# Output projections with each tile's evacuation one product later, full and partial tiles in turn, and VectorE in source order in layer A

## The chip, the core and the metric

One core of one Trainium2 chip runs the whole program. The metric is device time in microseconds (us) of one execution. Five engines work from queues of their own: TensorE (PE in the profile, its weight loads PEld), VectorE (DVE), ScalarE (ACT), GpSimd (POOL) and SyncE (SP), which issues most DMAs.

## What is computed

One inference step of a two-layer decoder over 1024 prompt tokens and 8 sample tokens. Layer A mixes tokens with a gated recurrence, layer B with sliding-window attention; both add a cross-attention into memory tokens. Around the change only this part of each layer matters:

```python
mix = jnp.concatenate([tok_out, x_out], axis=-1) @ w_out[l]
h = h + rms_norm(mix, norm_post_mix[l])
u = jnp.square(jax.nn.relu(rms_norm(h, norm_pre_mlp[l]) @ w_up[l]))
h = h + rms_norm(u @ w_down[l], norm_post_mlp[l])
```

The first line is the output projection. Width is 1024, so `w_out` has 8 output tiles of 128 features and 8 inner blocks of 128.

## The kernel before

Activations lie with features on the partitions. The 1032 tokens are cut into NCH = 3 chunks of CH = 344 columns. `X` holds the input of the current product, split into a high and a low part, so each inner block costs three matmuls (`mm3`, lines 287 to 289). A **full** tile of the projection is 8 blocks, 24 matmuls. A **partial** tile (`rest`) takes only the blocks that an earlier stage left out and is added to what that stage put into `Y[m]`: in layer A the two blocks LATE = (4, 5), 6 matmuls, for tiles 0 to 3; in layer B three blocks, 9 matmuls, for tiles 0 to 3 of chunks 0 and 1 (in chunk 2 all tiles are full).

A product lands in a PSUM bank and must be evacuated before the bank is used again. A full tile is evacuated by ScalarE (`A.copy` to `Y[m]`), a partial tile by VectorE (`tt(V, y, y, ps, add)`). Behind either stands `sumsq`: ScalarE squares the tile (line 221), and VectorE or GpSimd adds the square to the chunk's sums. Banks: layer A's projection takes "ax" (4 banks) and "dn" (2) in turn, layer B's only "dn".

After the last tile of a chunk, `post_norm` puts 12 pieces of work into the list `bg`: `stat` (loads of the residual `h`, matmuls of line 177 over the sums, square root, reciprocal, `spread`), `stat_b` (the matmul of line 197 that gives the scale to all partitions), eight `step(k)` and `stat_next` (line 177 again, over the squares of the new residual). `tick()` runs the next pieces: 1.5 of them after each tile of the following chunk, so that the norm of chunk c is traced among the products of chunk c + 1. The norm of the last chunk is traced among the first products of the MLP (`mlp`, `dense_chunk` with `up_ev`, line 1067), which read the X that the steps write, chunk by chunk. One step is this:

```python
V.scalar_tensor_tensor(y, y, gain(gpost, k), box["r"], op0=ALU.mult, op1=ALU.mult)
tt(V if k % 4 == 3 else G, y, y, h, ALU.add)
...
A.activation(h, y, AF.Square)
if k % 4 and not direct:
    r = row(k - k % 4)
    tt(V if k < 4 else G, r, r, h, ALU.add)
...
split_gain(y, gain(nxt, k), hi, lo)
```

`split_gain` is a ScalarE copy with a scale (hi) and a VectorE operation that subtracts it (lo).

A scheduler orders each engine's instructions by their readiness in its own estimate of time and by source order; where `ordered[0]` is set, the wrapper `InOrder` pins each VectorE instruction behind the one traced before it on VectorE. Before, it is set only inside `mlp`. Operations through `tt` are recorded on line 51 (VectorE) or line 98 (GpSimd).

Of the kernel before, what the change touches and what calls it, by code (L numbers as in the profile page):

```python
# [13 lines left out]
ALU = mybir.AluOpType  # L14
# [4 lines left out]
KT = D // P  # L19
# [3 lines left out]
CH = 344  # L23
NCH = 3
# [3 lines left out]
G_MEM, G_LB, G_HG, G_KV, G_PREMIX, G_POSTMIX, G_PREMLP, G_POSTMLP = 0, 16, 22, 28, 36, 52, 68, 84  # L28
# [6 lines left out]
def trunk_kernel(ctx, tc, xT, memT, wia, wib, wkk, wkv, wmk, wo, wu, wd, cmk, cmv, sth, ssk, ssv,  # L35
# [3 lines left out]
    ordered = [False]  # L39
# [15 lines left out]
    V, A, T, G, S = nc.vector, nc.scalar, nc.tensor, nc.gpsimd, nc.sync  # L55
    V = InOrder(V)
# [28 lines left out]
    def const(shape, name, src=None, dt=F32):  # L85
        t = cpool.tile(list(shape), dt, name=name, tag=name)
        if src is not None:
            S.dma_start(t, src)
        return t
# [7 lines left out]
    def tt(eng, out, a, b, op):  # L97
        return eng.tensor_tensor(out, a, b, op=op)  # L98
# [16 lines left out]
    def cs(c):  # L115
        return slice(c * CH, (c + 1) * CH)
# [99 lines left out]
    def sumsq(acc, src, first, eng):  # L216
        if first:
            A.activation(acc, src, AF.Square)
        else:
            sq = chunk_tile(acc.shape[-1])  # L220
            A.activation(sq, src, AF.Square)
            tt(eng, acc, acc, sq, ALU.add)
# [75 lines left out]
    def dense_mm(w, c, ks=range(KT), bank=None):  # L298
        ps = (psum(bank) if bank else dense_bank())[:, :CH]
        ks = list(ks)  # L300
        for i, k in enumerate(ks):
            mm3(ps, w[0][:, k * P:(k + 1) * P], w[1][:, k * P:(k + 1) * P], X[:, k, 0, cs(c)], X[:, k, 1, cs(c)],
                i == 0, i == len(ks) - 1)
        return ps

    def dense_chunk(w, c, evac, ks=range(KT)):
        evac(c, dense_mm(w, c, ks))
# [559 lines left out]
    def tick(n=1.5):  # L867
        due[0] += n
        while due[0] >= 1:
            due[0] -= 1  # L870
            if bg:
                bg.pop(0)()

    u2 = const([RB, N // RB], "u2")
    u4 = const([RB, N // RB], "u4")

    def post_norm(Y, a, w, acc, gpost, hsrc, hdst, nxt, scaled, bank="ac", rbank="ax", direct=False):

        hts, box = [], {}
        per = N // w
        sl, bl = slice(a, a + w), slice(a // RB, (a + w) // RB)

        def row(k):
            return hts[k // per][:, k % per]

        def stat():
            for i, k0 in enumerate(range(0, KT, per)):  # L890
                ht = slot("p" if i < 2 else "t", (P, per, w))
                n = min(per, KT - k0)
                for src, o in rows(hsrc, k0, n, a, w):
                    S.dma_start(ht[:, :n, o], src)
                hts.append(ht)
            st = rstd_tok(acc, square=u4[:, bl] if scaled else None, bank=rbank)
            if scaled:
                tt(V, st, st, u2[:, bl], ALU.mult)
            box["r"] = spread(st)

        def stat_b():
            box["r"] = bcast(box["r"], bank)

        def step(k):
            y, h = Y[k][:, sl], row(k)
            V.scalar_tensor_tensor(y, y, gain(gpost, k), box["r"], op0=ALU.mult, op1=ALU.mult)
            tt(V if k % 4 == 3 else G, y, y, h, ALU.add)
            for dst, o in rows(hdst, k, 1, a, w):
                S.dma_start(dst, y[:, o].unsqueeze(1))
            if nxt is None:  # L910
                return
# [4 lines that stand above are left out]
            hi, lo = X[:, k, 0, sl], X[:, k, 1, sl]  # L916
            if scaled:
                split(y, hi, lo, G if k % 4 == 1 else V)
            else:
                split_gain(y, gain(nxt, k), hi, lo)  # L920

        def stat_next():
            if nxt is None:
                return
            st = rstd_tok(*(row(k) for k in range(0, KT, 1 if direct else 4)), bank=rbank)
            if scaled:
                box["n"] = spread(st)
            else:
                tt(V, u2[:, bl], st, st, ALU.mult)
                tt(V, u4[:, bl], u2[:, bl], u2[:, bl], ALU.mult)  # L930

        def next_b():
            if nxt is not None and scaled:
                A.copy(nxt[:, sl], bcast(box["n"], bank))
        bg.extend([stat, stat_b] + [lambda k=k: step(k) for k in range(KT)] + [stat_next, next_b])
# [36 lines left out]
    def out_late(l, box, ws, hsrc, hdst):  # L972
        Y = box["Y"]
        accs = slot("t", (P, NCH, CH))
        Y += [slot(t) for t in ("q", "q", "k", "k")]

        def full(m, c):
            def ev(c, ps):
                A.copy(Y[m][:, cs(c)], ps)
                sumsq(accs[:, c], Y[m][:, cs(c)], m == ME, G if m % 2 else V)  # L980
            dense_chunk(ws[1 + m - ME], c, ev, ks=EARLY + LATE)

        def rest(m, c):
            ps = dense_bank()[:, :CH]
            w = ws[0]
            for i, k in enumerate(LATE):
                o = m * 256 + i * P
                mm3(ps, w[0][:, o:o + P], w[1][:, o:o + P], X[:, k, 0, cs(c)], X[:, k, 1, cs(c)], i == 0, i == 1)
            y = Y[m][:, cs(c)]
            tt(V, y, y, ps, ALU.add)  # L990
            sumsq(accs[:, c], y, False, V if m % 2 else G)

        wide[0] = True
        for c in range(NCH):
            for m in (4, 5, 6, 7, 0, 1, 2, 3):
                (full if m >= ME else rest)(m, c)
                tick()
            post_norm(Y, c * CH, CH, accs[:, c], G_POSTMIX + 8 * l, hsrc, hdst, G_PREMLP + 8 * l, False)
        return Y

    def out_b(hsrc, hdst):


        Y, ws, held, seen, box = {}, {}, {}, set(), {}
        first = EARLY[:5]

        def load(c, ks):
            for k in ks:
                n = CH if c < NCH - 1 or k > 5 else NP_ - c * CH
                t = held[k, c] = chunk_tile(n)  # L1010
                S.dma_start(t, mixs[k][:, c * CH:c * CH + n])

        def put(c, ks):
            for j, k in enumerate(ks):
                t = held[k, c]
                put_x(k, slice(c * CH, c * CH + t.shape[1]), t, G if j else V)

        def weight(m, tags=None):
            ws[m] = load_folded(12 + m, tags)

        def out(m):
            if m not in Y:
                Y[m] = slot("k" if m < 2 or m > 3 else "c")
            return Y[m]

        def stat(m, c):
            if "acc" not in box:
                box["acc"] = slot("r", (P, NCH, CH))
            sumsq(box["acc"][:, c], Y[m][:, cs(c)], c not in seen, V if m % 2 else G)
            seen.add(c)  # L1030

        def early(m, c):
            dense_chunk(ws[m], c, lambda c, ps: A.copy(out(m)[:, cs(c)], ps), ks=first)

        def rest(m, c):
            y = Y[m][:, cs(c)]
            tt(V, y, y, dense_mm(ws[m], c, EARLY[5:] + LATE), ALU.add)
            stat(m, c)

        def full(m, c):  # L1040
            dense_chunk(ws[m], c, lambda c, ps: A.copy(out(m)[:, cs(c)], ps), ks=EARLY + LATE)
            stat(m, c)

        def norm(c):
            post_norm([Y[m] for m in range(KT)], c * CH, CH, box["acc"][:, c], G_POSTMIX + 8, hsrc, hdst,
                      G_PREMLP + 8, False)
        return load, put, weight, early, rest, full, norm, Y
# [848 lines left out]
    def at(i, f, *args):  # L1896
        fill.setdefault(i, []).append(lambda: f(*args))
# [25 lines left out]
        for f in fs:  # L1923
            at(i, f)
    for i, f, m, c in ((23, early, 0, 0), (24, early, 1, 0), (25, early, 2, 0), (26, early, 0, 1), (27, early, 1, 1), (28, early, 2, 1), (29, early, 3, 0), (30, early, 3, 1), (29, rest, 0, 0), (30, rest, 1, 0), (30, rest, 2, 0), (31, rest, 3, 0), (32, full, 4, 0)):
        at(i, f, m, c)
    for i, *h in parts:
        at(i, load, *h)
    run_groups(groups, fill)
    weight(6, ("c", "c"))  # L1930
    weight(7, ("r", "r"))
    for c in range(NCH):
        for m in (*range(3, KT), *range(3)):
            if c or m > 4:
                (full if m > 3 or c == 2 else rest)(m, c)
                tick()
        norm(c)
    mlp(1, hs[2], yT, None, [YB[m] for m in range(KT)])
    tick(len(bg))

# [101 lines left out]
```

## Time and profile before

| what | value |
|---|---|
| median of 3 runs | 2524.55 us (2521.96 to 2527.94) |
| the profiled execution | 2523.64 us |
| its span | 2521.5 us |
| TensorE busy | 2342.8 us |
| VectorE busy | 1757.5 us |
| GpSimd busy | 1435.6 us |
| ScalarE busy | 1108.2 us |
| mean granted TensorE clock | 0.969 |

The span runs from the first to the last instruction of the profiled execution; 2.1 us of its time lie around it. Matmuls are pipelined, so a busy TensorE is not one at its peak. The output projection of layer A lies at about 580 to 653 us of the span, that of layer B at about 1,740 to 1,812 us.

### The profile page before, as it was taken

What the parts mean: (1) busy time and instruction counts of PE and PEld (TensorE: products, weight loads), DVE (VectorE), ACT (ScalarE), POOL (GpSimd) and SP (SyncE); (2) the same over time, 40 slices, a digit from 0 to 9 for tenths busy, and PEclk for the clock granted to TensorE, in tenths of its full rate; (3) what the DMA queues carried; (4) which work ended last, traced back from release to release, by engine and by line L of the source; (5) the groups of instructions that cost most, each with busy time, mean ns of one, the idle gap of its engine ahead of it and who ended that gap; (6) DMA issues with size and microseconds to landing.
All of it is one profiled execution on the core that took longest, in us unless ns stands there. A gap on an engine that the chain in (4) does not pass through costs nothing. (4 is left out here: it accounts for less than half of the span.)

```text
span 2521.5 us, 45361 instructions
## 1 busy us (share of the span) xinstructions
PE 2342.8 (93%) x17055; PEld 2261.5 (90%) x17055; DVE 1757.5 (70%) x2813; ACT 1108.2 (44%) x2457; POOL 1435.6 (57%) x1130
## 2 busy tenths in 40 slices
PE   7998999989899999999999998889999999899997
PEld 6887989989799999899998987778999999899997
DVE  7778677775768887567657466775577887567847
ACT  6573434444443333444344364565443333344424
POOL 4546453453686664557765344443576666457846
PEclk9999999999899999999999999889999999999998
DMA  4435455522335557655563333334334556755482
GB/s 160 134 103 183 159 186 160 169 86 91 107 118 177 175 184 240 191 161 151 194 213 106 118 88 114 101 94 148 109 105 157 184 173 202 257 147 153 127 280 75
DMA packets 231928, 383.01 MB, mean 152 GB/s; under 512 B 28106, under 2 KB 118794, under 8 KB 231692
## 3 DMA queue, kind: packets, MB, share of 16 engines
q1 hardware_dynamic: 154524, 253.80, 30.1%
q10 hardware_dynamic: 77184, 126.31, 17.2%
q8 instruction: 134, 2.20, 0.4%
q14 instruction: 86, 0.70, 0.1%
HBM read 253.27 MB, written 123.56 MB: 149 GB/s over the span
## 5 line engine op out<-in xcount | busy, mean ns | idle before, releaser
L287 PE MATMUL dn<-X,ws 128*128 128x344 f32 (+2 forms) x1136 | 374.2, 330 | 31.5 <-DVE X L51 10.7
L288 PE MATMUL dn<-X,ws 128*128 128x344 f32 (+2 forms) x1136 | 369.7, 325 | 0.0
L289 PE MATMUL dn<-X,ws 128*128 128x344 f32 (+2 forms) x1136 | 368.6, 324 | 0.0
L98 POOL TENSOR_TENSOR ws<-wr,ws 128x512 fp32r<-128x512 f32 (+1 forms) x118 | 223.6, 1897 | 160.8 <-ACT ws L225 146.4
L287 PEld LDWEIGHTS dn<-X,ws 128*128 128x128 f32 x1136 | 219.6, 193 | 42.3 <-DVE X L51 22.0
L51 DVE TENSOR_TENSOR X<-ws,X 128x516 fp32r<-128x516 f32 x160 | 172.7, 1088 | 105.8 <-ACT X L225 105.7
L288 PEld LDWEIGHTS dn<-X,ws 128*128 128x128 f32 x1136 | 219.9, 194 | 2.0 <-issue 0.8
L289 PEld LDWEIGHTS dn<-X,ws 128*128 128x128 f32 x1136 | 219.9, 194 | 1.2 <-issue 0.4
L287 PE MATMUL ax<-X 128*128 128x258 f32 x736 | 209.6, 286 | 9.9 <-DVE k L51 6.5
L288 PE MATMUL ax<-X 128*128 128x258 f32 x736 | 211.2, 287 | 4.2 <-POOL X L98 4.2
L289 PE MATMUL ax<-X 128*128 128x258 f32 x736 | 210.4, 286 | 0.0
L225 ACT CAST ws<-wr 128x1024 fp32r<-128x1024 f32 (+1 forms) x138 | 116.1, 844 | 132.8 <-DMA wfd<-ws 36.6
L98 POOL TENSOR_TENSOR p<-p,sm 128x512 f32<-128x512 f32 (+2 forms) x92 | 87.8, 977 | 130.4 <-DVE sm L51 72.8
L225 ACT CAST X<-ws 128x516 fp32r<-128x516 f32 (+1 forms) x192 | 109.6, 621 | 107.8 <-PE ax L289 45.6
L287 PEld LDWEIGHTS ax<-X 128*128 128x128 f32 x736 | 141.1, 192 | 10.9 <-DVE k L51 7.0
L287 PE MATMUL ax<-X,ws 128*128 128x344 f32 (+2 forms) x472 | 147.7, 314 | 2.6 <-DVE X L51 2.6
L289 PE MATMUL ax<-X,ws 128*128 128x344 f32 (+2 forms) x472 | 146.3, 310 | 0.0
L288 PEld LDWEIGHTS ax<-X 128*128 128x128 f32 x736 | 141.8, 193 | 5.0 <-POOL X L98 5.0
L288 PE MATMUL ax<-X,ws 128*128 128x344 f32 (+2 forms) x472 | 145.5, 308 | 0.0
L289 PEld LDWEIGHTS ax<-X 128*128 128x128 f32 x736 | 141.7, 193 | 0.0
L287 PE MATMUL ac<-X 128*128 128x258 f32 x496 | 139.5, 283 | 1.7 <-ACT k L1234 1.7
L288 PE MATMUL ac<-X 128*128 128x258 f32 x496 | 140.5, 284 | 0.0
(649 smaller groups left out, 8271.0 us busy)
## 6 DMA issues: line engine op xcount, KB each, us to landing
ws<-u ACTq DMA_DIRECT2D x160, 258.0 KB, 2.7
u<-k SPq DMA_DIRECT2D x104, 258.0 KB, 3.0
wr<-wu ACTq DMA_DIRECT2D x104, 256.0 KB, 3.3
wfd<-ws SPq DMA_DIRECT2D x20, 1024.0 KB, 5.1
X<-u21s SPq DMA_DIRECT2D x32, 516.0 KB, 6.8
ct<-u ACTq DMA_DIRECT2D x112, 129.0 KB, 2.8
u<-k SPq DMA_DIRECT2D x104, 129.0 KB, 2.3
u21s<-mv SPq DMA_DIRECT2D x26, 516.0 KB, 3.6
```

Source lines behind the costliest of these rows:

```text
L51: r = f(*args, **kw)
L98: return eng.tensor_tensor(out, a, b, op=op)
L225: A.copy(hi, src)
L287: T.matmul(ps, wh, xl, start=first, stop=False, skip_group_check=more)
L288: T.matmul(ps, wl, xh, start=False, stop=False, skip_group_check=more)
L289: T.matmul(ps, wh, xh, start=False, stop=last, skip_group_check=more)
```

## The change

Evacuation becomes a function of its own. `full` and `rest` now issue the matmuls and return the evacuation; the new `one_late` runs each evacuation after the next tile's matmuls have been traced, and then `tick()`. `norm(c)` is held back with the evacuation of the chunk's last tile, so it too stands behind the first product of the next chunk. Tiles go (4, 0, 5, 1, 6, 2, 7, 3) in place of (4, 5, 6, 7, 0, 1, 2, 3) in layer A and (3, 4, 5, 6, 7, 0, 1, 2) in layer B, where chunk 0 has only tiles 5, 6 and 7 left. In layer A `ordered[0]` is set for the whole of the three chunks, the steps of the norms of chunks 0 and 1 among them; in layer B it is not. The number of operations and their engines stay.

```diff
+    def one_late(o, steps):
+        ordered[0] = o
+        held = []
+        for f in steps:
+            if held and f.__defaults__[0] is None:
+                held.append(f)
+                continue
+            new = f()
+            for g in held:
+                g()
+            held = [new]
+            tick()
+        for g in held:
+            g()
+        ordered[0] = False
...
         def full(m, c):
-            def ev(c, ps):
+            ps = dense_mm(ws[1 + m - ME], c, EARLY + LATE)
+
+            def ev():
                 A.copy(Y[m][:, cs(c)], ps)
                 sumsq(accs[:, c], Y[m][:, cs(c)], m == ME, G if m % 2 else V)
-            dense_chunk(ws[1 + m - ME], c, ev, ks=EARLY + LATE)
+            return ev
...
-            y = Y[m][:, cs(c)]
-            tt(V, y, y, ps, ALU.add)
-            sumsq(accs[:, c], y, False, V if m % 2 else G)
+
+            def ev():
+                y = Y[m][:, cs(c)]
+                tt(V, y, y, ps, ALU.add)
+                sumsq(accs[:, c], y, False, V if m % 2 else G)
+            return ev
...
-        for c in range(NCH):
-            for m in (4, 5, 6, 7, 0, 1, 2, 3):
-                (full if m >= ME else rest)(m, c)
-                tick()
-            post_norm(Y, c * CH, CH, accs[:, c], G_POSTMIX + 8 * l, hsrc, hdst, G_PREMLP + 8 * l, False)
+        one_late(True, [(lambda m=m, c=c: (full if m >= ME else rest)(m, c)) if m is not None else lambda m=None, c=c: norm(c)
+                  for c in range(NCH) for m in (4, 0, 5, 1, 6, 2, 7, 3, None)])
...
-    for c in range(NCH):
-        for m in (*range(3, KT), *range(3)):
-            if c or m > 4:
-                (full if m > 3 or c == 2 else rest)(m, c)
-                tick()
-        norm(c)
+    one_late(False, [(lambda m=m, c=c: (full if m > 3 or c == 2 else rest)(m, c)) if m is not None
+              else lambda m=None, c=c: norm(c)
+              for c in range(NCH) for m in (4, 0, 5, 1, 6, 2, 7, 3, None) if c or m is None or m > 4])
```

In layer B `full`, `rest` are changed in the same way; its early tiles, run during the attention, still evacuate at once.

## Rows read from the trace of the kernel before

**Rows 1.** The page, busy time, share of the span and instructions of each engine.
```profile
PE 2342.8 (93%) x17055; PEld 2261.5 (90%) x17055; DVE 1757.5 (70%) x2813; ACT 1108.2 (44%) x2457; POOL 1435.6 (57%) x1130
```

**Rows 2.** Stretches of layer A: busy time (x instructions) of PE, PEld, DVE, ACT, POOL; clock.
```profile
596.10:622.20 26.10, 24.17 (x158) 23.67 (x156) 17.33 (x27) 12.35 (x29) 12.82 (x13) 1.00 0.20 68
622.20:653.30 31.10, 21.89 (x125) 20.89 (x125) 23.28 (x35) 16.01 (x35) 19.86 (x15) 0.79 0.49 166
653.30:687.00 33.70, 31.83 (x198) 30.70 (x198) 23.00 (x36) 12.61 (x28) 17.95 (x18) 0.94 0.24 79
```

**Rows 3.** TensorE's waits, 575 to 700 us: us in total, times, longest.
```profile
PE ax L177 <- DVE p L51: 5.9, 2, 3.9
PE dn L287 <- DVE k L51: 5.3, 1, 5.3
```

**Rows 4.** TensorE in order of time, layer A: start, us, instruction.
```profile
601.13 0.70 PE L177 MATMUL ax<-ones,t 128*86 128x1 f32 x8
...
606.02 0.74 PE L197 MATMUL ac<-ct,ones 86*128 86x344 f32 x2
...
612.40 0.32 PE L287 MATMUL ax<-X,p 128*128 128x344 f32 x1
...
616.20 0.32 PE L287 MATMUL dn<-X,ws 128*128 128x344 f32 x1
...
686.99 0.43 PE L287 MATMUL ax<-X,ws 128*128 128x344 f32 x1 [0.79 <-DVE X L51]
```

**Rows 5.** VectorE in order of time, layer A: evacuation, statistics, steps.
```profile
593.49 0.51 DVE L51 TENSOR_TENSOR k<-k,ax 128x344 f32<-128x344 f32 x1 [3.13 <-PE ax L289]
...
602.16 0.17 DVE L51 RECIPROCAL sm<-sm 86x4 f32<-86x4 f32 x1 [4.12 <-ACT sm L183]
602.37 0.51 DVE L51 TENSOR_TENSOR ct<-ident,sm 86x344 f32<-86x344 f32 x1
606.80 2.02 DVE L51 SCALAR_TENSOR_TENSOR k<-k,gn,ac 128x344 f32<-128x344 f32 x4 [3.93 <-PE ac L197]
...
613.99 0.57 DVE L51 SCALAR_TENSOR_TENSOR X<-k,gn,X 128x344 fp32r<-128x344 f32 x1
...
636.34 2.02 DVE L51 SCALAR_TENSOR_TENSOR k<-k,gn,ac 128x344 f32<-128x344 f32 x4 [3.91 <-PE ac L197]
...
668.58 2.02 DVE L51 SCALAR_TENSOR_TENSOR k<-k,gn,ac 128x344 f32<-128x344 f32 x4 [3.93 <-PE ac L197]
...
685.34 1.59 DVE L51 SCALAR_TENSOR_TENSOR X<-k,gn,X 128x344 fp32r<-128x344 f32 x1
```

**Rows 6.** ScalarE and GpSimd in order of time: square root, addition, square, hi part.
```profile
601.87 0.26 ACT L183 ACTIVATE sm<-ax,eps 86x4 f32<-86x4 f32 x1 [0.82 <-PE ax L177]
...
606.86 0.93 POOL L98 TENSOR_TENSOR t<-t,ct 128x344 f32<-128x344 f32 x1 [9.44 <-ACT ct L221]
...
608.71 0.49 ACT L912 ACTIVATE p<-k 128x344 f32<-128x344 f32 x1 [1.93 <-POOL k L98]
609.11 0.57 ACT L229 ACTIVATE X<-k,gn 128x344 fp32r<-128x344 f32 x1
```

**Rows 7.** DMA issues, 590 to 700 us: KB each, median us to landing.
```profile
p<-xT SPq DMA_DIRECT2D x4, 516.0 KB, 6.1
```

**Rows 8.** GpSimd's split of a weight and VectorE beside it, in order of time.
```profile
645.24 2.63 POOL L98 TENSOR_TENSOR ws<-wr,ws 128x1024 fp32r<-128x1024 f32 x1
...
645.58 2.66 DVE L51 TENSOR_TENSOR p<-p 128x344 f32<-128x344 f32 x1
```

**Rows 9.** Layer B, in order of time: an evacuation by VectorE, and TensorE.
```profile
1769.37 0.50 DVE L51 TENSOR_TENSOR k<-k,dn 128x344 f32<-128x344 f32 x1
1769.55 0.42 PE L177 MATMUL ax<-ones,p 128*86 128x1 f32 x2 [5.06 <-issue]
...
1770.27 0.49 PE L288 MATMUL dn<-X,ws 128*128 128x344 f32 x1
1770.55 0.49 PE L289 MATMUL dn<-X,ws 128*128 128x344 f32 x1
```

More of the change, by code (lines that the diff above doesn't have):

```diff
@@ L988, in rest, with norm @@
                 mm3(ps, w[0][:, o:o + P], w[1][:, o:o + P], X[:, k, 0, cs(c)], X[:, k, 1, cs(c)], i == 0, i == 1)
-            y = Y[m][:, cs(c)]
-            tt(V, y, y, ps, ALU.add)
-            sumsq(accs[:, c], y, False, V if m % 2 else G)
-        wide[0] = True
-        for c in range(NCH):
-            for m in (4, 5, 6, 7, 0, 1, 2, 3):
-                (full if m >= ME else rest)(m, c)
-                tick()
-            post_norm(Y, c * CH, CH, accs[:, c], G_POSTMIX + 8 * l, hsrc, hdst, G_PREMLP + 8 * l, False)
+            def ev():
[3 more added lines that the diff above has]
+            return ev
+        def norm(c):
+            post_norm(Y, c * CH, CH, accs[:, c], G_POSTMIX + 8 * l, hsrc, hdst, G_PREMLP + 8 * l, False)
+        wide[0] = True
+        one_late(True, [(lambda m=m, c=c: (full if m >= ME else rest)(m, c)) if m is not None else lambda m=None, c=c: norm(c)
+                  for c in range(NCH) for m in (4, 0, 5, 1, 6, 2, 7, 3, None)])
         return Y
@@ L1035, in rest, with ev @@
         def rest(m, c):
-            y = Y[m][:, cs(c)]
-            tt(V, y, y, dense_mm(ws[m], c, EARLY[5:] + LATE), ALU.add)
-            stat(m, c)
-        def full(m, c):
-            dense_chunk(ws[m], c, lambda c, ps: A.copy(out(m)[:, cs(c)], ps), ks=EARLY + LATE)
-            stat(m, c)
+            ps = dense_mm(ws[m], c, EARLY[5:] + LATE)
+            def ev():
+                y = Y[m][:, cs(c)]
+                tt(V, y, y, ps, ALU.add)
+                stat(m, c)
+            return ev
+        def full(m, c):
+            ps = dense_mm(ws[m], c, EARLY + LATE)
+            def ev():
+                A.copy(out(m)[:, cs(c)], ps)
+                stat(m, c)
+            return ev
         def norm(c):
@@ L1925, in trunk_kernel @@
     for i, f, m, c in ((23, early, 0, 0), (24, early, 1, 0), (25, early, 2, 0), (26, early, 0, 1), (27, early, 1, 1), (28, early, 2, 1), (29, early, 3, 0), (30, early, 3, 1), (29, rest, 0, 0), (30, rest, 1, 0), (30, rest, 2, 0), (31, rest, 3, 0), (32, full, 4, 0)):
-        at(i, f, m, c)
+        at(i, f if f is early else lambda f, *a: f(*a)(), *(() if f is early else (f,)), m, c)
     for i, *h in parts:
```

## The prediction

> **What bounds the kernel now.** The page comes first: TensorE is busy 93% of the span [rows 1], so a change that adds and removes no work can only move TensorE's idle stretches and the moment from which it runs without a gap. The stretches of layer A come next: from 596.1 to 687.0 us, 90.9 us, TensorE is busy 24.17 + 21.89 + 31.83 = 77.9 us, 13.0 us idle, and in the middle stretch its granted clock is 0.79 [rows 2]. TensorE's waits name what is late: 5.9 us in two waits of line 177 (the statistics of the new residual, `stat_next`) for VectorE, and 5.3 us in one wait for a bank that VectorE has not evacuated [rows 3]. In layer B one wait of line 177 takes 5.06 us, put down to "issue"; VectorE's instruction that starts 0.18 us before its end, an evacuation of a partial tile, shows which queue was behind [rows 9]. So 16 us of TensorE's idle time hang on VectorE.
>
> They are not all a gain, though. Follow VectorE in layer A: the first scaling of the three norms starts at 606.80, 636.34 and 668.58, and the last lo part of the third ends at 685.34 + 1.59 = 686.93 [rows 5]; TensorE, in the third chunk of the MLP's first products, is waiting for it and goes on at 686.99 [rows 4]. From there it runs without a wait. Layer A's time is therefore set by when VectorE ends the third norm; TensorE reaching that point sooner only waits longer. In layer B the stretch after the 5.06 us wait is TensorE's own, and a wait removed there is kept.
>
> **Layer A, part by part.** The later evacuation and the new order add no operation. Two things change for the chain of norms.
>
> First, `stat_b` now has a partial tile in front of it in source order, where a full one stood. Four partial tiles take 616.20 - 612.40 = 3.80 us, so a partial tile costs 0.95 and a full one, four times the matmuls, 3.80 [rows 4]. From line 177 to line 197 it is 606.02 - 601.13 = 4.89 us now; 2.85 less gives 2.04, about what the chain between needs: 0.70 for the matmuls, 0.26 square root, 0.17 reciprocal, 0.51 spread [rows 4, 5, 6]. The first norm starts at 606.80 - 2.85 = 603.95.
>
> Second, VectorE's source order. Before, VectorE did all eight scalings in a row and the lo parts behind them, while GpSimd and ScalarE worked on the steps between. Pinned, the lo part of step k stands ahead of the scaling of step k + 1, so a step runs as a chain: scaling 0.51 (2.02 for four), addition on GpSimd 0.93, square 0.40 (608.71 to 609.11, when ScalarE takes the next), hi part 0.57, lo part 0.57 [rows 5, 6]; with four hand-overs of about 0.03 us 3.1 us. The two steps whose addition is VectorE's own take 0.51 in place of 0.93: 2.7. Eight steps: 6 x 3.1 + 2 x 2.7 = 24.0 us. Between them stand the evacuations: two of 0.5, one addition of 0.5, and one that also waits for ScalarE's square, 0.5 + 0.49 + 0.5 = 1.5 (an evacuation is 0.51 [rows 5]): 3.0. Together 27.0 us.
>
> Then `stat_next`: 16 matmuls of line 177, twice the 0.70, square root, reciprocal and two small products of about 0.16: 2.15; and the last partial tile with its square, 1.5. The next norm's sums are then ready, and `stat` and `stat_b` take 0.70 + 0.26 + 0.17 + 0.51 + 0.74 = 2.4. By this sum a period is 27.0 + 2.15 + 1.5 + 2.4 = 33.05. The residual's loads give more: their places are free only when `stat_next` has read the squares in them, and they land 6.1 us after the issue [rows 7], ahead of the first addition: 27.0 + 1.4 + 6.1 - 0.5 = 34.0. I take 34.0, since the next norm now follows at once; the periods before were 29.54 and 32.24 [rows 5].
>
> Second norm: 603.95 + 34.0 = 637.95. Its VectorE work and the last evacuation end 27.0 + 2.15 + 1.5 later, at 668.6. The third norm is outside the pinned stretch, its `stat_b` still behind a full tile: 4.89 + 0.78 (606.02 to 606.80) = 5.67 later, 674.27, against 668.58. Its 18.35 us are as before. The end of layer A's chain moves by **+5.7 us**. The waits of rows 3 may go (evacuations come early in VectorE's queue), but their time turns into a longer wait for X.
>
> Bounds: if line 177 runs as soon as the sums are there, the first norm starts some 3 us earlier still, at 600.6, and two periods of 33.05 with the short 2.4 for the third norm too give 666.7, -1.9. Upwards GpSimd stands in the chain: three weight splits for the MLP fall into chunk 2, each some 2.4 us or, as in rows 8, 2.63; in front of an addition each may cost its whole length, +7.2, so +12.9.
>
> One row here has a rule beside it. VectorE's 128x344 operation at 645.58 takes 2.66 us, not 0.5, and starts 0.34 us after a GpSimd split of 2.63 [rows 8]. The Trainium skill (SBUF — State Buffer, "Who interferes with whom") says that VectorE operations with two SBUF inputs and GpSimd share a port pair that is locked for a whole instruction, so whoever comes second blocks. The trace agrees (2.66 beside 2.63). By that rule a pinned VectorE stands still under each split with all that is queued behind it, which is the slower rival below; a VectorE that waits for GpSimd's addition anyway no longer collides with it, which is the 0.57 taken above.
>
> **Layer B, part by part.** VectorE stays free there, so no step becomes a chain. With two banks, the product after next needs the bank that VectorE has to evacuate. The partial tiles stood last in the chunk, one behind another, where VectorE was 5.06 us behind [rows 9]; now each has a full tile's 3.80 us as cover before its bank is wanted. Left: 5.06 - 3.80 = 1.26 us. Behind the wait 12 matmuls ran 0.28 us apart (1770.27 to 1770.55) in place of 0.16, the lower of the clock's two levels (1.2 GHz), 1.5 us, which go with it. Together **-5.3 us**. Bounds: 0, if the wait is one for the steps and not for banks; -6.6, if all goes.
>
> The order of the full tiles, and weight slots freed later in chunk 2 (tile 7 is now next to last), cost nothing: the third weight of the MLP is wanted two full products, 7.6 us, after the first. Without that cover it would be a cast and a split, about 3.7 us.
>
> **Sum.** 2523.64 + 5.7 - 5.3 = 2524.0 for the profiled execution, which lies 0.9 us under the median of the runs shown: **2525 us**.
>
> **Rivals.**
> *The chain is not the bound (faster).* If the steps overlap enough that a pinned period stays as before, layer A keeps the two shorter ways to `stat_b`, 2 x 2.85 = -5.7, and B its -5.3: 2524.55 - 11.0 = 2513.5. For it: VectorE is busy only 23.28 of 31.10 us in the chunk where it holds TensorE up [rows 2], and its operations run at 0.5 us when GpSimd is still. Against: the lo part needs the hi part, whatever the engines' shares.
> *GpSimd's splits stand in the chain (slower).* With +7.2 A is +12.9, B -5.3: 2524.55 + 7.6 = 2532. For it: rows 8. Against: the scheduler may put the splits elsewhere. It decides from two splits in the chain on.
> *The change does not do in layer B what it says.* The wait is line 177's for the squares of the steps, which the order of tiles does not shorten: B 0, A +5.7: 2530. For it: the waiting instruction is line 177, not a product. Against: the evacuations stand beside its end.
>
> **How the numbers follow.** The forecast 0.36, the faster rival 0.34, the splits 0.18, no gain in B 0.12. This kernel can tell about 0.2%, 5 us, from no change, so the forecast is "same", and the last two are slower. The range is to hold the faster rival's 2513.5 and the splits' 2532, and a little on each side for the bounds (-1.9 and -6.6 make 2516; a clock less low in layer A, with no wait left, some 1.5 below the faster rival): 2512 to 2534. The likeliest case's own range is 2520 to 2529.
>
> **What would show it.** Right: in layer A scalings of one step each, 3 us apart, none in a row of four; the second and third norm starting near 638 and 674; TensorE's waits for line 177 and the bank gone or short and a longer idle time ahead of the third chunk's X; in layer B no wait over 2 us between 1750 and 1775. Wrong: norm periods of 30 us or less in A (the faster rival), a VectorE operation of over 2 us inside the pinned steps (the slower one), or a wait of line 177 of 4 us or more still in B. The forecast would fail altogether if TensorE, not X, were late at the third chunk.

## The result, and the profile after

| kernel | median | runs | ratio to before, 95% interval |
|---|---|---|---|
| before | 2522.64 us (2510.86 to 2527.94) | 6 | |
| changed | 2549.68 us (2546.92 to 2554.31) | 6 | 1.0115 [1.0097, 1.0133] |

By the medians the change costs 27 us, 1.07%, a little less than the ratio of 1.0115 says; the forecast was 2525 in a range that ended at 2534. The profiled execution of the changed kernel took 2549.19 us, its span 2547.4, the mean granted clock 0.966. Lines of the changed kernel have moved: 979 is 999, 912 is 930; lines 51, 98, 177, 197, 229, 287 and 289 are where they were.

The page, busy time by engine, as in [rows 1]:

```profile
PE 2347.7 (92%) x17055; PEld 2263.7 (89%) x17055; DVE 1755.5 (69%) x2815; ACT 1109.6 (44%) x2457; POOL 1427.7 (56%) x1128
```

No engine has more work; the span is 26 us longer by waiting. The stretches of layer A show where, with columns as in [rows 2]:

```profile
596.10:622.20 26.10, 24.28 (x157) 23.50 (x156) 10.07 (x19) 9.34 (x21) 5.69 (x6) 1.00 0.08 28
622.20:653.30 31.10, 21.58 (x116) 20.72 (x116) 11.02 (x21) 10.19 (x21) 13.15 (x11) 0.73 0.29 93
653.30:687.00 33.70, 15.82 (x84) 14.92 (x83) 17.66 (x30) 11.72 (x25) 14.97 (x15) 0.74 0.30 108
687.00:715.30 28.30, 24.52 (x138) 23.21 (x137) 19.37 (x27) 11.53 (x26) 15.74 (x16) 0.89 0.26 88
```

In [rows 2] VectorE was busy 23.28 of the 31.10 us of the second stretch; now 11.02. It has not become faster: the work has spread over a fourth stretch of 28.3 us. No engine is full in the two middle stretches, which is what a chain across engines looks like. TensorE's granted clock is down to 0.73 and 0.74 there.

TensorE's waits from 575 to 700 us, against [rows 3]:

```profile
PE ax L177 <- POOL p L98: 16.7, 2, 10.2
PE dn L288 <- POOL ws L98: 3.5, 1, 3.5
PE dn L287 <- ACT ws L225: 2.8, 1, 2.8
PE ax L177 <- DVE t L51: 2.5, 1, 2.5
PE dn L287 <- DVE k L51: 1.4, 1, 1.4
```

The bank's wait of 5.3 us is down to 1.4, as meant. The long waits of line 177 have grown from 5.9 to 16.7 us and name another engine, and there are shorter ones for VectorE beside them. VectorE in order of time shows one whole period (first scaling of a norm to first scaling of the next), against [rows 5]:

```profile
607.42 0.57 DVE L51 SCALAR_TENSOR_TENSOR k<-k,gn,ac 128x344 f32<-128x344 f32 x1 [3.91 <-PE ac L197]
610.11 0.57 DVE L51 SCALAR_TENSOR_TENSOR X<-k,gn,X 128x344 fp32r<-128x344 f32 x1 [2.11 <-ACT X L229]
610.60 0.50 DVE L51 TENSOR_TENSOR k<-k,ax 128x344 f32<-128x344 f32 x1
611.03 0.56 DVE L51 SCALAR_TENSOR_TENSOR k<-k,gn,ac 128x344 f32<-128x344 f32 x1
613.15 0.70 DVE L51 TENSOR_TENSOR p<-p 128x344 f32<-128x344 f32 x1 [1.56 <-ACT p L930]
613.78 1.24 DVE L51 SCALAR_TENSOR_TENSOR X<-k,gn,X 128x344 fp32r<-128x344 f32 x1
614.94 0.56 DVE L51 SCALAR_TENSOR_TENSOR k<-k,gn,ac 128x344 f32<-128x344 f32 x1
...
635.92 0.98 DVE L51 SCALAR_TENSOR_TENSOR X<-k,gn,X 128x344 fp32r<-128x344 f32 x1 [1.03 <-ACT X L229]
...
640.73 0.52 DVE L51 TENSOR_TENSOR t<-t,ct 128x344 f32<-128x344 f32 x1 [0.62 <-ACT ct L221]
642.96 0.17 DVE L51 RECIPROCAL sm<-sm 86x4 f32<-86x4 f32 x1 [1.71 <-ACT sm L183]
643.17 0.51 DVE L51 TENSOR_TENSOR ct<-ident,sm 86x344 f32<-86x344 f32 x1
649.62 0.57 DVE L51 SCALAR_TENSOR_TENSOR k<-k,gn,ac 128x344 f32<-128x344 f32 x1 [5.94 <-PE ac L197]
...
680.00 1.10 DVE L51 SCALAR_TENSOR_TENSOR X<-k,gn,X 128x344 fp32r<-128x344 f32 x1 [1.03 <-ACT X L229]
...
686.07 0.52 DVE L51 TENSOR_TENSOR t<-t,ct 128x344 f32<-128x344 f32 x1 [0.62 <-ACT ct L221]
...
696.62 2.02 DVE L51 SCALAR_TENSOR_TENSOR k<-k,gn,ac 128x344 f32<-128x344 f32 x4 [3.93 <-PE ac L197]
...
713.17 2.09 DVE L51 SCALAR_TENSOR_TENSOR X<-k,gn,X 128x344 fp32r<-128x344 f32 x2
```

Scaling, a wait of 2.11 us for GpSimd and ScalarE, lo part, next scaling: the rows of four scalings are gone from the two pinned norms (the third, which is not pinned, still has one). Three parts make a period: the steps (607.42 to 635.92 + 0.98 = 636.90, 29.5 us), the way to the next norm's sums (to 640.73 + 0.52 = 641.25, 4.35), and from the sums to the first scaling (to 649.62, 8.4). The second period has 31.5 (649.62 to 681.10), 5.5 (to 686.59) and 10.0. The last lo part of the third norm ends at 715.26, against 686.93: 28.3 us later. ScalarE's first copy of line 1234 (now 1265), in the MLP behind it, stands at 770.4 against 741.9, 28.5 later, the whole span ends 25.9 later. So layer A loses 28.3 and 2.4 come back behind it.

TensorE in order of time, around the sums and the scale of the first, the second and the third norm:

```profile
601.76 0.70 PE L177 MATMUL ax<-ones,t 128*86 128x1 f32 x8
...
606.64 0.74 PE L197 MATMUL ac<-ct,ones 86*128 86x344 f32 x2
...
636.58 2.21 PE L177 MATMUL ax<-ones,p 128*86 128x1 f32 x14 [6.48 <-POOL p L98]
641.30 1.33 PE L177 MATMUL ax<-ones,t 128*86 128x1 f32 x8 [2.51 <-DVE t L51]
642.49 0.64 PE L287 MATMUL ax<-X,ws 128*128 128x344 f32 x1
642.92 0.49 PE L288 MATMUL ax<-X,ws 128*128 128x344 f32 x1
643.21 0.49 PE L289 MATMUL ax<-X,ws 128*128 128x344 f32 x1
...
648.66 0.35 PE L287 MATMUL ax<-X,ws 128*128 128x344 f32 x1
648.84 0.74 PE L197 MATMUL ac<-ct,ones 86*128 86x344 f32 x2
...
685.50 0.66 PE L287 MATMUL dn<-X,ws 128*128 128x344 f32 x1 [1.37 <-DVE k L51]
...
690.94 0.70 PE L177 MATMUL ax<-ones,t 128*86 128x1 f32 x8
...
695.84 0.74 PE L197 MATMUL ac<-ct,ones 86*128 86x344 f32 x2
```

In the second norm the spread is ready at 643.17 + 0.51 = 643.68. Line 197 runs at 648.84, because 22 matmuls of a full product stand in front of it in TensorE's queue, and they come 0.29 us apart in place of 0.16: the lower of the clock's two levels (1.2 GHz). The granted clock was 1.00 up to 631 us, fell while TensorE stood 6.48 us at line 177, and was 0.50 from 632 to 648. In the third norm the sums are ready at 686.59, but line 177 runs at 690.94, behind a product that waited for a bank and started at the lower level (14 of its 22 matmuls in front of line 177 come 0.29 us apart).

### The profile page after: what moved, and what is told of

It reads as the page before. It is cut to its first block, busy times and chain, and to the rows that moved or that the text cites. A ratio compares the mean times of both kernels' runs of the same rounds, so it can differ in the third digit from the quotient of the medians.

```text
span 2547.4 us, 45351 instructions
## 1 busy us (share of the span) xinstructions
PE 2347.7 (92%) x17055; PEld 2263.7 (89%) x17055; DVE 1755.5 (69%) x2815; ACT 1109.6 (44%) x2457; POOL 1427.7 (56%) x1128
## 5 line engine op out<-in xcount | busy, mean ns | idle before, releaser
L287 PEld LDWEIGHTS dn<-X,ws 128*128 128x128 f32 x1136 | 220.4, 194 | 45.8 <-DVE X L51 26.4
```

The lines of the kernel that those rows point to most:

```text
L287: T.matmul(ps, wh, xl, start=first, stop=False, skip_group_check=more)
```

## The experiments

Theory: VectorE's pinned order makes every step of the first two norms a chain over three engines, layer A's end follows the third norm, and all else in the change is small. The rivals were the other parts of the change, TensorE's own order (its stand at `stat_next`) and GpSimd's weight splits. The table stands ahead, since one reading covers it: first scaling of the three norms and end of the last lo part in the profiled execution, the median, and its distance from the kernel before measured beside it (medians 2520.4 to 2522.6).

| run | norm 1 | norm 2 | norm 3 | last lo part ends | median us | against before |
|---|---|---|---|---|---|---|
| before | 606.80 | 636.34 | 668.58 | 686.93 | 2522.64 | |
| changed | 607.42 | 649.62 | 696.62 | 715.26 | 2549.68 | +27.0 |
| e1, all but the pin | 605.86 | 634.52 | 673.63 | 691.95 | 2525.06 | +2.6 |
| e2, the pin alone | 607.71 | 649.26 | 692.88 | 711.54 | 2544.14 | +21.7 |
| e3, layer B alone | 603.68 | 631.26 | 663.66 | 682.04 | 2522.49 | 0.0 |
| e5, steps overlapped | 607.14 | 639.26 | 675.90 | 694.55 | 2523.82 | +1.4 |
| e6, no stat_next | 601.79 | 641.37 | 684.52 | 703.19 | 2536.60 | +16.2 |
| e6b, before, no stat_next | 606.87 | 632.25 | 658.61 | 677.25 | 2511.57 | -8.8 |
| e7, splits as copies | 606.38 | 649.01 | 695.02 | 713.68 | 2550.47 | +30.1 |
| e8, late alone | 603.95 | 633.46 | 665.98 | 684.34 | 2521.03 | +0.6 |
| e9, statistics behind | 603.89 | 634.36 | 662.84 | 681.68 | 2524.04 | +1.7 |
| e10, the same and B | 605.99 | 635.48 | 663.96 | 682.78 | 2524.38 | +2.0 |
| e12, scale at once | 604.91 | 642.12 | 687.99 | 706.88 | 2537.18 | +14.8 |
| e15, no splits | 604.99 | 647.46 | 692.62 | 711.26 | 2541.61 | +20.1 |

Wherever the last lo part ends 16 us or more later than in the kernel before, the median is later by as much, within 6 us; where it ends within 8 us of it, the median is within 3 us of no change; e6b, 9.7 us earlier, is 8.8 us faster. That fits layer A's end being set by VectorE's third norm, over fourteen kernels. One execution scatters by several us, so the small differences of the table say little.

**e1 and e2: the pin away, and the pin alone.**

```diff
e1, in the changed kernel:
-        one_late(True, [(lambda m=m, c=c: (full if m >= ME else rest)(m, c)) if m is not None else lambda m=None, c=c: norm(c)
+        one_late(False, [(lambda m=m, c=c: (full if m >= ME else rest)(m, c)) if m is not None else lambda m=None, c=c: norm(c)
e2, in the kernel before:
+        ordered[0] = True
         for c in range(NCH):
...
+        ordered[0] = False
```

> The change whole, but VectorE not pinned in layer A. Theory (the pin makes each step of a norm a chain, and nearly all of layer A's 28 us of delay hangs on it): the third norm's first scaling in layer A goes back from 696.6 to 665 to 672 us, and the time comes within 10 us of the kernel before or below it, that is 25 us or more below the changed kernel. Rival (the later evacuations and the alternating order themselves put the norms off): the third norm starts after 685 and the time stays at least 15 us above the kernel before.

> The kernel before with nothing but VectorE pinned to source order over layer A's three chunks. Theory (the pin alone costs it): 20 to 35 us above the kernel before, scalings one per step and some 3 us apart, periods of the norms of 40 us or more. Rival (the pin costs only together with late evacuations and alternating tiles): within 8 us of the kernel before.

e1: 2525.06, ratio 1.0006 [0.9993, 1.0019]. e2: 2544.14, 1.0082 [1.0061, 1.0104]. The pin is the loss: 21.7 us without the new order, 24.6 (2549.68 - 2525.06) with it. In e1 the third norm starts at 673.63, a little behind the 665 to 672 expected. Late evacuation and new order do not gain what was hoped of them either. In e1 TensorE's waits from 575 to 700 us are these:

```profile
PE ax L177 <- issue: 16.2, 2, 12.0
PE dn L287 <- DVE X L51: 4.0, 2, 3.2
```

The bank's wait is gone and line 177 waits 16.2 us, with nothing to show for it in the time: TensorE's waits by themselves are not the bound here.

**e3 and e8: layer B's change alone; the late evacuation alone.** e8 is e1 with the tiles in the old order.

```diff
e8, in e1:
-                  for c in range(NCH) for m in (4, 0, 5, 1, 6, 2, 7, 3, None)])
+                  for c in range(NCH) for m in (4, 5, 6, 7, 0, 1, 2, 3, None)])
...
-              for c in range(NCH) for m in (4, 0, 5, 1, 6, 2, 7, 3, None) if c or m is None or m > 4])
+              for c in range(NCH) for m in (3, 4, 5, 6, 7, 0, 1, 2, None) if c or m is None or m > 4])
```

> Layer A as before, layer B as changed. By the landmarks of the two traces layer B gave back some 2 to 4 us of layer A's delay, so theory: 1 to 5 us below the kernel before, perhaps too little to measure. My prediction's own term was -5.3. Rival (layer B's order is neutral or worse, and the 2.4 us came from elsewhere in the program): at or above the kernel before.

> The late evacuation alone: the tiles in the order of the kernel before in both layers, VectorE not pinned. With late evacuation and alternation together and no pin the time was 2525.1 against 2522.5. Theory (both are neutral by themselves): 2519 to 2527, the norms of layer A starting near 606, 636 and 670. Rival (one gains what the other loses): late evacuation alone costs 5 us or more, since the evacuation of a tile stands behind the norm's steps, or alone gains 5 us or more.

e3: 0.9996 [0.9981, 1.0011]; e8: 0.9990 [0.9974, 1.0005]. Neither part can be measured; the 1 to 5 us expected of e3 did not come. e8's first norm starts at 603.95, but e3, whose layer A is the old one, has 603.68: three us of that landmark are no effect of the change.

**e5: the pin kept, the steps overlapped.** The second half of a step (the sum of squares, hi and lo part) is traced behind the first half of the step after next, so that VectorE has other scalings to do while GpSimd and ScalarE work.

```diff
-        bg.extend([stat, stat_b] + [lambda k=k: step(k) for k in range(KT)] + [stat_next, next_b])
+        def both(k):
...
+            step(k)
+            if k >= 2:
+                finish(k - 2)
+            if k == KT - 1:
+                finish(k - 1)
+                finish(k)
+        bg.extend([stat, stat_b] + [lambda k=k: both(k) for k in range(KT)] + [stat_next, next_b])
```

> The change whole, pin included, but in the pinned stretch the second half of step k (VectorE's sum of squares and the hi and lo parts) is traced behind the first half of step k + 2, so that VectorE has other steps' scalings to do while GpSimd and ScalarE work. Theory (the loss is the chain inside a step): the steps of a norm take some 20 us instead of 29.5 and 31.5, TensorE's two long waits for the statistics shrink, and the time falls by 12 to 28 us below the changed kernel. Rival (the loss is TensorE's order: a product between the two statistics matmuls at the lower clock, whatever the steps take): less than 8 us below the changed kernel.

2523.82, ratio 1.0006 [0.9990, 1.0022]: 25.9 us come back with the pin still there. VectorE in order of time:

```profile
607.14 0.57 DVE L51 SCALAR_TENSOR_TENSOR k<-k,gn,ac 128x344 f32<-128x344 f32 x1 [3.91 <-PE ac L197]
607.63 0.51 DVE L51 TENSOR_TENSOR k<-k,ax 128x344 f32<-128x344 f32 x1
608.05 1.05 DVE L51 SCALAR_TENSOR_TENSOR k<-k,gn,ac 128x344 f32<-128x344 f32 x2
609.99 0.90 DVE L51 SCALAR_TENSOR_TENSOR X<-k,gn,X 128x344 fp32r<-128x344 f32 x1 [0.90 <-ACT X L229]
610.82 0.56 DVE L51 SCALAR_TENSOR_TENSOR k<-k,gn,ac 128x344 f32<-128x344 f32 x1
611.42 0.65 DVE L51 TENSOR_TENSOR k<-k,p 128x344 f32<-128x344 f32 x1
...
623.98 2.40 DVE L51 SCALAR_TENSOR_TENSOR X<-k,gn,X 128x344 fp32r<-128x344 f32 x2
```

A wait of 0.90 us for a hi part, where the changed kernel waits up to 2.11 in a step; the steps end at 623.98 + 2.40 = 626.38, after 19.2 us in place of 29.5. TensorE's waits for GpSimd at line 177 shrink with them, from 16.7 to 3.8 us. The second norm still has 7.06 us between line 177 (631.42) and line 197 (638.48), so the rival of TensorE's order is not what came back here. What costs is not the program order but what was traced in that order.

**e6 and e6b: `stat_next` left out**, in the changed kernel and in the kernel before.

```diff
         def stat_next():
...
+            if not scaled and hsrc is hsA[0] and a < 2 * CH:
+                G.memset(u2[:, bl], 1.0)
+                G.memset(u4[:, bl], 1.0)
+                return
```

> The changed kernel, pinned, but the matmuls of stat_next (line 177 over the squares of the new residual), its square root, reciprocal and small products are left out for chunks 0 and 1 of layer A; constants stand in their place. In the changed kernel TensorE stands 6.48 and 10.23 us at these matmuls, its granted clock falls, and from the sums of the next norm to its first scaling it takes 8.4 and 10.0 us where the forecast had 2.4 and 5.67. Theory: the chain inside the steps is the cause, and TensorE's stand at stat_next is its second part: with nothing to stand at, the way from the sums to the scaling shortens by 3 to 5 us for each norm, the norms start some 35 to 39 us apart in place of 42 and 47, and the time is 2533 to 2541. Rival 1 (TensorE's order alone is the cause; the chain of steps would not matter without the stand): periods near 30 and 32 us, the time at the kernel before, 2523, or below. Rival 2 (the steps alone; the stand is hidden): periods stay at 41 to 46 us and the time at 2545 to 2550.

> The kernel before with the same work left out (stat_next of chunks 0 and 1 of layer A), as the measure for the run beside it. In it line 177 waits 5.9 us for VectorE in two waits. If layer A ends with VectorE's third norm, as the prediction has it, the waits taken away move little: 2518 to 2524. Rival (TensorE's waits count in full): 5.9 us and the matmuls go, 2514 to 2517.

e6: 2536.60, 1.0066 [1.0042, 1.0089]; e6b: 2511.57, 0.9957 [0.9940, 0.9973]. By its time e6 met the theory, but by luck: the term that the theory named did not come. From the sums to the first scaling it still takes 633.30 to 641.37 and 674.45 to 684.52, 8.1 and 10.1 us, and the periods are 39.6 and 43.2 us, not 35 to 39. The time came from shorter ways to the sums (1.6 us in place of 4.35 and 5.5) and a first norm 5.6 us earlier, for which no cause is shown. Its partner is a second warning: the same work left out of the kernel before brings 8.8 us, more than either expectation there. From e6b to e6 the change still costs 25.0 us, with no `stat_next` to stand at. So the stand there is a symptom of what the pin adds, not a second cause. In e6 the waits only move:

```profile
PE dn L287 <- DVE k L51: 14.0, 1, 14.0
PE ax L177 <- DVE t L51: 11.4, 1, 11.4
```

And e6b shows that the statistics of the new residual are in the chain from norm to norm of the kernel before as well: its periods fall from 29.5 and 32.2 to 25.4 and 26.4.

**e7 and e15: GpSimd's splits of the MLP's first three weights away**, as copies on ScalarE (e7) or without a substitute (e15).

```diff
e7, in load_w, for layer A's MLP's first three weights:
-        split(raw, hi, lo, G)
+        if plain:
+            A.copy(hi, raw)
+            A.copy(lo, raw)
+        else:
+            split(raw, hi, lo, G)
e15, in its place:
+        if plain:
+            A.copy(hi, raw)
+            return hi, hi
...
```

> The changed kernel, pinned; the lo part of the first three weights of layer A's MLP is not a subtraction on GpSimd of 2.3 to 2.9 us but a plain copy on ScalarE (the product is another one for it, its instructions the same in number). Theory: the splits lengthen the chain of steps by 2.5 us in the second chunk and 4.5 in the third, by holding VectorE (1.58 to 2.12 us for an operation of 0.5) and by standing ahead of an addition on GpSimd; without them the second and third period shrink by about as much, and the time is 2541 to 2546. Rival (the splits stand in the slack of the chain): the periods stay at 42 and 47, the time at 2547 to 2551. A larger gain than 10 us would say that the splits, not the chain inside a step, are the larger part of the loss.

> The changed kernel, pinned; the lo part of the first three weights of layer A's MLP is left out and nothing takes its place (the product reads the hi part twice, so its value is another one and its instructions are the same in number). In the run with copies on ScalarE in place of the splits, a step's square on ScalarE stood behind two casts of 1.05 us, so the price had only changed its engine. Theory (the splits lengthen the chain of steps by 2.5 us in the second chunk and 4.5 in the third): steps of 27 to 28 us from the first scaling to the end of the last lo part in place of 29.5 and 31.5, and 2541 to 2546. Rival (other waits hold the steps at that length, the splits lie in their slack): 29 to 31 us, and 2547 to 2552.

e7: 2550.47, 1.0105 [1.0075, 1.0136], no gain. ScalarE in order of time shows what e7 had changed; line 248 and 249 are the two copies, line 934 the square of a step:

```profile
629.14 1.05 ACT L248 CAST ws<-wr 128x1024 fp32r<-128x1024 f32 x1
630.08 1.05 ACT L249 CAST ws<-wr 128x1024 fp32r<-128x1024 f32 x1
631.03 0.49 ACT L934 ACTIVATE t<-k 128x344 f32<-128x344 f32 x1
```

The square waits for the copies, and VectorE 3.33 us for the hi part behind it, where it waited 2.08: in this chain a filler on ScalarE costs too. e15: 2541.61, 1.0085 [1.0061, 1.0110], inside the theory's range, but the stretches do not bear the theory out: the steps take 29.2 and 28.8 us (604.99 to 634.20, 647.46 to 676.23) in place of 29.5 and 31.5. The splits are worth 0.3 and 2.7 us there, not 2.5 and 4.5, and the last lo part ends 4.0 us earlier, while the median fell by 8. What the other 4 are was not found.

**e12: line 197 right behind line 177**, by pinning these matmuls and the first of the next products among each other. The expectation speaks of the second norm, but the edit holds for all three norms of layer A.

```diff
+        def stat_both():
+            pinned[0] = 1 << 30
+            stat()
+            stat_b()
+            pinned[0] = 5
...
+        inA = not scaled and hsrc is hsA[0]
+        bg.extend(([stat_both] if inA else [stat, stat_b]) + [lambda k=k: step(k) for k in range(KT)] + [stat_next, next_b])
```

> The changed kernel, pinned, with TensorE's matmul of line 197 (the scale to all partitions) right behind line 177 in the second norm of layer A; in the changed kernel a full product of 7.5 us at the lower level of the granted clock stands between them, and the norm's first scaling comes 8.4 us after its sums. In the first and third norm the products between stay where they are. Theory (this product is a term of the longer period of its own): the second norm starts 4 to 5.5 us earlier, the third follows by as much, and the time is 2543 to 2547. Rival (TensorE does the same products later and the chain meets them there): the third norm starts within 2 us of where it did, 2548 to 2552.

2537.18, 1.0059 [1.0040, 1.0078]: 12.5 us back, more than expected. TensorE around the second norm (line 183 is 177, 203 is 197, 294 is 288):

```profile
638.14 1.33 PE L183 MATMUL ax<-ones,t 128*86 128x1 f32 x8 [2.86 <-DVE t L51]
640.57 1.51 PE L203 MATMUL ac<-ct,ones 86*128 86x344 f32 x2 [1.10 <-DVE ct L51]
...
642.17 0.49 PE L294 MATMUL dn<-X,p 128*128 128x344 f32 x1
```

From VectorE's last sum (638.08) to the scaling it is 4.0 us in place of 8.4. In the third norm line 197 follows line 177 as well, and the way is 681.48 to 687.99, 6.5 us in place of 10.0; the product ahead of line 177 stays. In the first norm products stay between the two lines (599.72 to 604.13). With a first norm 2.5 us earlier that is 2.5 + 4.4 + 3.5 = 10.4, of which the steps and the way to the sums took 1.8 back; the third norm starts 8.6 us earlier and the last lo part ends 8.4 earlier; the other 4 us of the median are not accounted for.

**e9 and e10: looking for a better kernel.** In the kernel before, `stat_next` of chunks 0 and 1 stands behind the next norm's `stat_b`, with the squares added into a tile of their own (`later` is run there, `next_stat` is the old `stat_next`); e10 has layer B's change too.

```diff
...
+                t = chunk_tile(w)
+                tt(V, t, row(0), row(4), ALU.add)
+                later.append(lambda: next_stat(t))
+                return
```

> The kernel before, all work kept, but in layer A the second statistics of chunks 0 and 1 (line 177 over the squares of the new residual) stand behind the next norm's stat_b instead of ahead of its stat: VectorE adds the two rows of squares into a tile of their own (one addition more for each, 0.5 us), so that the residual's places come free without TensorE. Leaving this work out altogether brought 8.8 us (2511.6 against 2520.4) with norm periods of 25.4 and 26.4 us. Theory (the statistics stand in the chain from one norm to the next, and only their place matters): most of the 8.8 us, norm periods of 26 to 29 us, 2511 to 2517. Rival (the work itself is what costs, or the added addition and its wait take the place): periods stay near 30 and 32 us, 2518 to 2525.

> The run beside it with layer B as in the changed kernel (late evacuation, full and partial tiles in turn, not pinned), which by itself gave 2522.5 against 2522.5. Theory (layer B's part is worth 0 to 3 us): 0 to 3 us below the run beside it. Rival (the forecast's 5.3 us are there once layer A's end comes earlier): 5 us or more below it.

e9: 0.9998 [0.9985, 1.0012]; e10: 1.0004 [0.9992, 1.0016]. The theory fell: the periods are 30.5 and 28.5 us, the second shorter and the first not, and the time is that of the kernel before. Layer B's part again cannot be measured: e10 is 0.3 us above e9. No version beat both kernels with all of the work kept.

## Why the prediction was wrong

**What bounds layer A** was right. The end follows VectorE's third norm (the table), TensorE's longer waits cost nothing by themselves (e1), and the sign of layer A's part was that of the forecast.

**That pinned steps become chains** was right, and e5 shows it. The size was nearly right: 27.0 us of steps and evacuations were forecast, 29.5 and 31.5 measured. The step that starts at 614.94 takes 3.2 us to the next scaling at 618.10, against 3.1; the one before, with two operations made longer, 3.9. Splits are worth 0.3 and 2.7 of the excess (e15); in the rest are operations such as the 1.24 us at 613.78 beside an addition of GpSimd. The Trainium skill (SBUF — State Buffer, "Who interferes with whom") has a VectorE operation with two SBUF inputs and a GpSimd operation that reads SBUF block each other for a whole instruction; the trace agrees again, with an addition of 2.12 us on VectorE at 660.48 beside a split of 2.34 us on GpSimd from 659.88. The slower rival that drew on it was right in kind and small in size.

**The step that failed is the way from the sums to the next scaling**, put at 2.4 us for the second norm and 5.67 for the third; it measures 8.4 and 10.0, together 10.3 us of the miss. The forecast read TensorE's order from the source, with a partial tile between line 177 and line 197 where a full one had stood, 2.85 us less, and took line 197 as free to run when the spread was ready. But TensorE is not pinned, and its queue did not follow: 27 matmuls stand between the two lines in the first norm (601.76 to 606.64, 4.88 us against 4.89 before), 22 in the second and 27 in the third (4.90 us). So the first norm was put too early as well (603.95; it came at 607.42), 3.5 us more.

The second part of the same step is the clock. The forecast had seen that TensorE would wait longer, and put that at nothing; but the products behind a wait run at the lower level, inside the next norm's own chain. In the second norm this makes 7.54 us from line 177 to line 197. In the third these two lines are as far apart as forecast, and a product ahead of line 177 takes the 4.35 us from the sums (686.59) to it (690.94). That it was the wait at `stat_next` does not matter: without `stat_next` (e6) TensorE waits elsewhere and the ways are as long. e12 shows the part between the lines: the two ways shorten by 4.4 and 3.5 us. No run takes away the product ahead of line 177 in the third norm, so that part is read from the trace alone.

**Smaller terms.** From the last lo part to the sums 3.65 was put, 4.35 and 5.5 came. The residual's loads, put at 34.0 for the first period, did not bind. The sum of the miss at the third norm's start: 3.5 (first norm) + 2.5 + 4.5 (steps) + 0.7 + 1.85 (to the sums) + 6.0 + 4.3 (to the scaling) - 0.95 (loads) = 22.4, and 696.62 - 674.27 = 22.35.

**Layer B**: the forecast misread [rows 9], and its third rival was right about the wait. The evacuation that starts 0.18 us before line 177 ends at 1769.87, after line 177 has begun, so line 177 did not wait for it. It reads `p`, and VectorE's last addition to `p` ends 0.11 us before it starts:

```profile
1768.94 0.50 DVE L51 TENSOR_TENSOR p<-p,p 128x344 f32<-128x344 f32 x1
```

That is the squares of the steps, as in layer A. In the changed kernel line 177 still waits 2.10 us for VectorE's `p` (to 1822.23), and a product waits 1.77 us for VectorE (to 1793.27). These two take most of the 5.06 us; the landmarks give 2.4 us back of the 5.3 forecast, and e3 and e10 show nothing that can be measured.

**The faster rival**, that a pinned period stays as it was, fell by the first row: 42.2 us against 29.5. What stays open: alternation alone was not run, what sets TensorE's order between line 177 and line 197 was not varied apart from e12, and medians and landmarks differ by 4 to 7 us in e3, e5, e9, e10, e12 and e15 without a cause shown (in e3, e9 and e10 the profiled execution itself was 5 to 6 us faster than the median).

## What to carry to other kernels

Before an engine is put into source order, read what the source order is: a helper that traces scaling, addition, square and lo part of one item as a block is harmless where a scheduler may interleave items, and a chain over three engines where it may not; overlapping the items in the source (e5) gave back 25.9 us with the pin in place. When such a chain makes TensorE wait longer, do not book the wait as idle time that costs nothing: ask which of its queued products will then run late, and whether a short matmul of the next chain stands behind them. Read that queue from a trace and not from the source, where the engine is not pinned. And compare an experiment that leaves work out with the same cut in the kernel before, or a gain both would have is taken for proof.

## What the runs showed of the hardware

While TensorE stood at line 177 in the changed kernel, its granted clock fell from 1.00 to 0.50, and the product that followed ran its matmuls 0.29 us apart in place of 0.16: 22 of them took 6.35 us (642.49 to 648.84), where 24 take 3.80 at the upper level [rows 4]. A wait costs again after it has ended. The kernel before, unchanged, measured from 2510.9 to 2535.8 us over the runs of this study, so that parts worth under 3 us could not be told from nothing.
